# Hand-set engine order for the sample's MLP, four lasting two-bank PSUM tiles, down operands in three stages

## The chip, the cores and the metric

The kernel runs on one core of a Trainium2 chip. The metric is device time in microseconds (us) of one execution, the median of several runs. A core has engines with an instruction queue each: TensorE (PE in the profile, with its weight loads as PEld) multiplies matrices into PSUM, VectorE (DVE), ScalarE (ACT) and GpSimd (POOL) work elementwise, and SyncE (SP) issues most DMA transfers. Engines wait for each other on semaphores.

## The reference

One layer of an encoder is applied to two inputs with the same weights, a prompt of 512 rows and a sample of 1024 rows, width 1024. All is float32.

```
h = rmsnorm(x);  z = h @ w_in                       # q, k, v and two convolution inputs
a = window attention (128 to each side, relative bias, a sink logit per head)
c = silu(layernorm(depthwise conv over 31 rows of (ca * sigmoid(cb))))
x = x + concat(a, c) @ w_out
h = rmsnorm(x)
u = depthwise conv over 3 rows of (h @ w_up)         # 2 x 2816 columns: gate and value
x = x + (silu(u_gate) * u_value) @ w_down            # the MLP
y = rmsnorm(x)
```

The rows that matter here are the last four, for the sample.

## The kernel before

**Precision and products.** A float32 operand is split into a high part in the fast matmul format and a low part, the remainder (a cast on ACT, a subtraction on DVE or POOL). A product then takes three matmuls: high by high, high by low, low by high. Each is 128 x 128 by 128 x 512, or, for a transpose, 128 x 128 by 128.

**Until 907 us of the profiled execution** come the projections of both inputs (`proj`, L249 to L252: groups of matmuls into a PSUM bank, with `tick()` after each six, which lets other work be issued between), the convolution (`conv_items`: one scalar_tensor_tensor on DVE per tap, L292, which reads and writes an accumulator in a PSUM bank), attention (scores L501 to L524, values and their transposes L545 to L569), the convolution's norm (L604 to L624), the prompt's MLP (`up_half`: matmuls into two banks, then the centre tap on ACT, L778, and two outer taps on DVE, L774; `down`: L812 to L815) and the output projection (`out_half`, L640 to L645).

**PSUM.** In this part the PSUM is eight tiles of one bank (2 KB a partition), named a0 to a2, u0, u1, b0, b1 and c0 (L105). `use` (L109) says which letters a job may take: "step" (projections) takes a, u or b; the convolution's accumulator c; the prompt's up products u, its down products b. At 907 us this pool is closed, and a second pool of four tiles of two banks (`wide()`) serves the rest.

**The sample's MLP, from 907 us.** Both products use a scheme of seven products over halves, as Strassen's. The up product goes column block by column block: j from 0 to 21, each with a gate part x and a value part wy, each a wide tile with a left half L and a right half R. For a column the steps are `first` and `second` (into x left; `first` is also copied to a), `fourth` (x right), `sixth` then `seventh` (wy right, with sums u2 and u3 made from it on DVE, L915), `fifth` then `third` (wy left). Each is `prod`, 12 matmuls (L1042 to L1044). The rows of the normed x are transposed by `turned` (PE L965, cast on ACT L967, low part on DVE L918) in the start stage, and the up weights of column j come by DMA (`load_up`), are summed on DVE (`sums_up`, L918) and split (`split_up`: cast on ACT L1028, low part on POOL L918). Then come the depthwise convolution (centre on ACT L1140, two taps on DVE L1141 and L1142), the gate (tanh on ACT L1149, DVE L1159) and the product with the value (DVE L1161). The gated result of each pair of columns is written to DRAM in seven combinations (`ga`).

The down product is 77 steps, seven products over eleven pairs of columns. A step takes 12 matmuls (L1306 to L1308, `mm_down`), its operands are `ga` tiles and blocks of w_down, read again by `load_next`, with sums on DVE and splits on ACT, POOL and DVE (`operands`, made four steps ahead, `LEAD`). After each product `evacuate` adds the PSUM tiles into accumulators. `load_x1` loads the residual, `with_x` adds it. Behind the last product's steps stand the tail: add (L915), squares (`left_first` L1357, `finish` L1365), the reciprocal root on POOL (L1366 to L1368), scaling (L1372 to L1377) and the stores (L1378).

**What sets the order.** The code is written in an order, but the framework's scheduler rearranges the whole kernel's instructions on each engine before it is built (`schedule_with_timeline_sim=True`).

Of the kernel before, what the change touches and what calls it, by code (L numbers as in the profile page):

```python
# [15 lines left out]
P = 128  # L16
# [78 lines left out]

@with_exitstack
def tile_hybrid_encoder(ctx: ExitStack, tc: tile.TileContext, xs, rel_bias, norm_attn_g, w_in,
# [6 lines left out]
    ps_guard = tc.tile_pool(name="ps", bufs=1, space=bass.MemoryType.PSUM)  # L104
    ps = ps_guard.__enter__()  # L105
# [8 lines left out]
    def bank(job):  # L114
        return banks.tile([NT], among=use[job])
# [887 lines left out]

    def sums_up(j):
        if j < NJ:
            g0, g1, v0, v1 = (block_up(j, half, k) for half in range(2) for k in range(2))
            t = third_sum[j] = sb.tile([NT])
            sub(t[:], v1, v0, nc.gpsimd)
            sub(v0, v0, g0)
            sub(g0, v1, v0)  # L1010
            sub(g1, g1, g0)
# [70 lines left out]
    out_blocks(NB - 1, 1)  # L1082
# [3 lines left out]
    gFb = None  # L1086
# [4 lines left out]
    def wide():  # L1091
        return wide_banks.tile([W2])
# [5 lines left out]
    def first(j):  # L1098
        if j < NJ:
            s = st[j] = dict(x=wide(), a=sb.tile([NT]))  # L1100
            prod(s["x"][:, L], j, 1, True, True)
            nc.scalar.copy(s["a"][:], s["x"][:, L])
# [4 lines left out]
    def sixth(j):  # L1107
        s = st[j]
        s["wy"] = wide()
        s["u2"] = sb.tile([NT])  # L1110
        prod(s["wy"][:, R], j, 6, True, True)
        add(s["u2"][:], s["wy"][:, R], s["a"][:])

    def fourth(j, between=None):
        prod(st[j]["x"][:, R], j, 4, True, True, between)

    def seventh(j):
# [12 lines left out]

    def third(j):
        s = st[j]
        W = s["wy"][:, L]
        prod(W, j, 3, False, True)
        add(W, W, s.pop("u2")[:])

    def dwconv(src, f):
        w = lambda t: fw[:, t * 44 + f:t * 44 + f + 1]
        u = sb.tile([W2])
        nc.scalar.activation(u[:], src[:], AF.Identity, scale=w(1), bias=fb[:, f:f + 1])  # L1140
        nc.vector.scalar_tensor_tensor(u[:, 1:W2], src[:, 0:W2 - 1], w(0), u[:, 1:W2], op0=ALU.mult, op1=ALU.add)  # L1141
        nc.vector.scalar_tensor_tensor(u[:, 0:W2 - 1], src[:, 1:W2], w(2), u[:, 0:W2 - 1], op0=ALU.mult, op1=ALU.add)  # L1142
        return u

    def gate_part(j):
        s = st[j]
        ug = s["ug"] = dwconv(s.pop("x"), j)
        t = s["t"] = sb.tile([W2])
        nc.scalar.activation(t[:], ug[:], AF.Tanh, scale=0.5)  # L1149
# [3 lines left out]
    def value_part(j):  # L1153
        if j < 0:
            return
        p = j // 2
        s = st.pop(j)
        ug, t = s["ug"], s["t"]
        nc.vector.scalar_tensor_tensor(t[:], t[:], 1.0, ug[:], op0=ALU.add, op1=ALU.mult)  # L1159
        uv = dwconv(s.pop("wy"), NJ + j)  # L1160
        nc.vector.tensor_tensor(t[:], t[:], uv[:], op=ALU.mult)  # L1161
        del ug, uv
        s.clear()
        if j % 2 == 0:
            even[p] = t
            nc.sync.dma_start(ga[1, p][:], t[:, L])
            return
        e, x, y = even.pop(p), sb.tile([W2]), sb.tile([NT])
        for i, blk in ((2, L), (4, R)):
            nc.sync.dma_start(ga[i, p][:], t[:, blk])  # L1170
        add(x[:, R], e[:, R], t[:, R])
        sub(x[:, L], e[:, L], e[:, R], nc.gpsimd)
        sub(e[:, R], x[:, R], e[:, L])
        sub(y[:], t[:, L], e[:, R], nc.gpsimd)
        for i, b in ((5, x[:, R]), (7, x[:, L]), (6, e[:, R]), (3, y[:])):
# [3 lines left out]
    def halves():  # L1179
        while True:  # L1180
            t = wide()
            yield t, t[:, L]
            yield t, t[:, R]
            t = None

    two = halves()

    def turn(i):
        return turned(i, lambda: next(two))

    first(0)
    first(1)
    t = turn(4)
    next(t)
    second(0, t)
    for _ in t:
        pass
    t = turn(6)
    next(t)
    second(1, t)  # L1200
    for _ in t:
        pass
    split_up(0, 7)
    t = turn(7)
    next(t)
    fourth(0, t)
    for _ in t:
        pass
    split_up(1, 7)
    t = turn(5)  # L1210
    next(t)
    fourth(1, t)
    for _ in t:
        pass
    split_up(0, 5)
    for _ in turn(3):
        pass
    two.close()
    reserve(2)
    load_up(2, 0)  # L1220
    load_up(2, 1)
    split_up(1, 5)
    sixth(0)
    split_up(0, 3)
    sixth(1)
    split_up(1, 3)
    seventh(0)
    load_up(3, 0)
    seventh(1)
    load_up(3, 1)  # L1230
    fifth(0)
    split_up(2, 1, 2)
    sums_up(2)
    fifth(1)
    gate_part(0)
    third(0)
    split_up(2, 6, 4)
    value_part(0)
    first(2)
    gate_part(1)  # L1240
    third(1)
    split_up(2, 7, 5, 3)
    load_up(4, 0)
    load_up(4, 1)


    pr = {}
# [24 lines left out]
    hl = {}  # L1272

    def operands(i, p):

# [236 lines left out]
```

## Time and profile before

| | us |
|---|---|
| median of 3 runs | 1614.8 (1608.98 to 1616.14) |
| profiled execution, its whole time | 1616.81 |
| profiled execution, span from first to last instruction | 1615.0 |
| granted TensorE clock, mean | 0.984 |
| instructions on PE, DVE, ACT, POOL | 6907, 1681, 1358, 673 |
| HBM read, written | 158.84 MB, 48.51 MB |

The profile comes from one execution on the chip. A row of a group reads: line, engine, operation, output and inputs by the names of their buffers, shape, count; then the busy time of the group in us, the mean of one in ns, the time for which the engine was idle just before them, and the instruction that ended most of it. In rows by time the idle time and its releaser stand in square brackets. Matmuls overlap, so that the pitch, the time from one's start to the next one's start, is shorter than the duration shown for one.

### The profile page before, as it was taken

To read this page: it belongs to the slowest core of one execution; us is meant where nothing else is said; L and a number is where in the kernel's file an instruction comes from. 1 tells how busy PE (TensorE), PEld (TensorE's weight loads), DVE (VectorE), ACT (ScalarE), POOL (GpSimd) and SP (SyncE) were. 2 spreads that over 40 slices of the span, in tenths; PEclk is the share of its full clock that TensorE was granted. 3 is DMA by queue.
4 is the path that set the end of the run, shared out by engine and by line. 5 is a ranking of instruction groups with operands and counts; after the bars stand their busy time and mean duration, and the time that the engine had idled before them with its cause. 6 is when DMAs were issued, how large, how long until landed. Compare 5 with 4: busy or idle time off the path is not lost. (4 is left out here: it accounts for less than half of the span.)

```text
span 1615.0 us, 20218 instructions
## 1 busy us (share of the span) xinstructions
PE 1540.5 (95%) x6907; PEld 1243.8 (77%) x6907; DVE 1201.1 (74%) x1681; ACT 762.5 (47%) x1358; POOL 882.8 (55%) x673
## 2 busy tenths in 40 slices
PE   8999899999999999999999999999999999999995
PEld 6778788877877878888678767787777787878774
DVE  7999857749899987666656658777777776786685
ACT  4634656255556665555543334333343344344353
POOL 6641344157656866555622335656666664555586
PEclk9999999999999999999999979999999999999998
DMA  7572256274233333334482212333333324974512
GB/s 234 154 208 76 79 134 176 82 205 129 82 101 105 111 103 100 105 98 156 150 261 85 66 53 85 98 98 98 98 98 98 98 79 176 320 262 159 166 51 104
DMA packets 209772, 207.63 MB, mean 129 GB/s; under 512 B 11156, under 2 KB 150748, under 8 KB 209541
## 3 DMA queue, kind: packets, MB, share of 16 engines
q1 hardware_dynamic: 209669, 206.35, 40.6%
q8 instruction: 54, 0.88, 0.2%
q14 instruction: 49, 0.40, 0.1%
HBM read 158.84 MB, written 48.51 MB: 128 GB/s over the span
## 5 line engine op out<-in xcount | busy, mean ns | idle before, releaser
L918 POOL TENSOR_TENSOR q<-q,q 128x512 fp32r<-128x512 f32 x107 | 147.3, 1387 | 138.7 <-ACT q L1028 138.6
L1042 PE MATMUL w<-h,q 128*128 128x512 f32 x516 | 203.5, 397 | 10.8 <-DVE h L915 4.6
L143 POOL TENSOR_TENSOR q<-q,q 128x1024 fp32r<-128x1024 f32 x72 | 175.1, 2436 | 68.6 <-ACT q L142 37.5
L1044 PE MATMUL w<-h,q 128*128 128x512 f32 x516 | 201.2, 394 | 0.8 <-POOL q L918 0.8
L1043 PE MATMUL w<-h,q 128*128 128x512 f32 x494 | 194.6, 394 | 0.0
L918 DVE TENSOR_TENSOR h<-h,h 128x512 fp32r<-128x512 f32 (+1 forms) x126 | 137.8, 1136 | 45.6 <-DMA h<-in_w_down 28.0
L249 PE MATMUL u<-h,q 128*128 128x512 f32 x400 | 159.5, 399 | 3.6 <-DVE h L774 2.8
L250 PE MATMUL u<-h,q 128*128 128x512 f32 x400 | 159.0, 397 | 0.6 <-DVE h L211 0.6
L252 PE MATMUL u<-h,q 128*128 128x512 f32 x384 | 151.8, 395 | 2.0 <-POOL q L143 1.8
L918 POOL TENSOR_TENSOR h<-h,h 128x512 fp32r<-128x512 f32 x69 | 104.9, 1536 | 86.0 <-ACT h L922 61.4
L292 DVE SCALAR_TENSOR_TENSOR c<-c,cvw,c 128x512 f32<-128x512 f32 x184 | 137.9, 750 | 2.4
L922 ACT CAST h<-h 128x512 fp32r<-128x512 f32 x154 | 87.3, 618 | 110.6 <-DVE h L918 39.2
L1042 PEld LDWEIGHTS w<-h,q 128*128 128x128 f32 x516 | 97.5, 189 | 38.9 <-issue 8.1
L1307 PE MATMUL w<-h,h 128*128 128x512 f32 x296 | 117.9, 398 | 7.6 <-DVE h L918 7.6
L1308 PE MATMUL w<-h,h 128*128 128x512 f32 x308 | 122.1, 398 | 0.7 <-POOL h L918 0.7
L1306 PE MATMUL w<-h,h 128*128 128x512 f32 x308 | 122.0, 397 | 0.0
L1044 PEld LDWEIGHTS w<-h,q 128*128 128x128 f32 x516 | 97.4, 189 | 23.8 <-POOL q L918 1.7
L1028 ACT CAST q<-q 128x512 fp32r<-128x512 f32 x107 | 65.1, 620 | 105.8 <-PE w L1044 51.7
L142 ACT CAST q<-q 128x1024 fp32r<-128x1024 f32 x72 | 75.6, 1050 | 77.7 <-POOL q L143 44.3
L1043 PEld LDWEIGHTS w<-h,q 128*128 128x128 f32 x494 | 93.4, 189 | 20.2
L249 PE MATMUL b<-h,q 128*128 128x512 f32 x256 | 102.1, 399 | 1.9 <-DVE d L322 1.9
L250 PE MATMUL b<-h,q 128*128 128x512 f32 x256 | 100.7, 393 | 0.0
(398 smaller groups left out, 3957.5 us busy)
## 6 DMA issues: line engine op xcount, KB each, us to landing
q<-in_w_up SPq DMA_DIRECT2D x88, 512.0 KB
h<-in_w_down SPq DMA_DIRECT2D x110, 256.0 KB
h<-ga SPq DMA_DIRECT2D x77, 256.0 KB
ga<-q SPq DMA_DIRECT2D x66, 256.0 KB
q<-in_w_in SPq DMA_DIRECT2D x28, 512.0 KB
q<-in_x_sample SPq DMA_DIRECT2D x15, 512.0 KB
h<-qsd SPq DMA_DIRECT2D x24, 256.0 KB
q<-in_x_prompt SPq DMA_DIRECT2D x8, 512.0 KB
```

Source lines behind the costliest of these rows:

```text
L143: (nc.vector if dve else nc.gpsimd).tensor_tensor(lo[:], raw[:], hi[:].bitcast(F32), op=ALU.subtract)
L249: nc.tensor.matmul(out, whi[:, kc, :], hi[:], start=(kc == 0), stop=False)
L250: nc.tensor.matmul(out, whi[:, kc, :], lo[:], start=False, stop=False)
L252: nc.tensor.matmul(out, wlo[:, kc, :], hi[:], start=False, stop=(kc == KC - 1))
L292: nc.vector.scalar_tensor_tensor(acc[:], src(t), w(t), acc[:], op0=ALU.mult, op1=ALU.add)
L918: (eng or nc.vector).tensor_tensor(out, a, b, op=ALU.subtract)
L1042: nc.tensor.matmul(out, whi[:, s], hi[:], start=(start and c == 0), stop=False, **go)
L1043: nc.tensor.matmul(out, whi[:, s], lo[:], start=False, stop=False, **go)
L1044: nc.tensor.matmul(out, wlo[:, s], hi[:], start=False, stop=(stop and c == 3), **go)
L1306: nc.tensor.matmul(out, sh[:, c], th[:], start=(p == 0), stop=False)
L1307: nc.tensor.matmul(out, sh[:, c], tl[:], start=False, stop=False)
L1308: nc.tensor.matmul(out, sl[:, c], th[:], start=False, stop=(p == NPAIR - 1))
```

## The change

It has three parts.

1. *PSUM.* The class `Banks` makes four tiles of two banks, w0 to w3, which last for the whole kernel. In the early part the old bank names are halves of them: w0 is b0 and a2, w1 is b1 and c0, w2 is a0 and a1, w3 is u0 and u1. The MLP takes whole tiles. The closing of the first pool and the second pool go.
2. *Order.* From the scaling of the last block of rows to the end, the code stands under `tc.manual_schedule()`: each engine runs its instructions in the order in which they are written. That order is rewritten: the start stage with its transposes, the loop over the columns, and the tail. Before it, in the early part, the scheduler still sets the order.
3. *Down operands.* Sums are made two steps ahead of the low parts, casts one ahead, and the lows some steps ahead of the matmuls (`advance`, 4 steps, more toward the end). Loads begin in the last three columns, into slots that the raw up weights leave.

```diff
+class Banks:
+    NAMES = (("b0", "a2"), ("b1", "c0"), ("a0", "a1"), ("u0", "u1"))
+    def __init__(self, pool):
+        self.tiles = [pool.tile([P, 2 * NT], F32, tag=f"w{i}", name=f"w{i}", bufs=1) for i in range(4)]
+        self.free = [f"{k}{i}" for k, n in (("a", 3), ("u", 2), ("b", 2), ("c", 1)) for i in range(n)]
+        self.wides = list(range(4))
+    def bank(self, among):
+        name = next((b for b in self.free if b[0] in among), None)
...
+        i, h = next((i, pair.index(name)) for i, pair in enumerate(self.NAMES) if name in pair)
+        return Bank(self.free, name, self.tiles[i][:, h * NT:(h + 1) * NT])
+    def wide(self):
+        i = self.wides.pop(0)
+        return Bank(self.wides, i, self.tiles[i][:, :])
...
-    banks = Slots(ps, dict(a=(3, 2048), u=(2, 2048), b=(2, 2048), c=(1, 2048)))
+    banks = Banks(ps)
...
-    ps_guard.__exit__(None, None, None)
-    ps2 = ctx.enter_context(tc.tile_pool(name="ps2", bufs=1, space=bass.MemoryType.PSUM))
-    wide_banks = Slots(ps2, dict(w=(4, 4096)))
...
     def seventh(j):
         s = st[j]
-        s["u3"] = sb.tile([NT])
         prod(s["wy"][:, R], j, 7, False, True)
-        add(s["u3"][:], s["wy"][:, R], s.pop("a")[:])
+        u3 = s["u3"] = sb.tile([NT])
+        add(u3[:], s["wy"][:, R], s.pop("a")[:])
+        add(s["x"][:, R], s["x"][:, R], u3[:])
 
     def fifth(j):
         s = st[j]
-        W, Y = s["wy"][:, L], s["wy"][:, R]
-        prod(W, j, 5, True, True)
-        u3 = s.pop("u3")
-        add(Y, W, u3[:])
-        add(s["x"][:, R], s["x"][:, R], u3[:])
+        prod(s["wy"][:, L], j, 5, True, True)
+        add(s["wy"][:, R], s["wy"][:, L], s.pop("u3")[:])
...
+    def down_casts(k):
+        for x in list(hl[k]):
+            hi = sb.tile([NT], F32R)
+            nc.scalar.copy(hi[:], x[:])
+            hl[k].append(hi)
+    def down_lows(k):
+        a, b, ah, bh = hl[k]
+        p = steps[k][1]
+        al, bl = sb.tile([NT], F32R), sb.tile([NT], F32R)
+        sub(al[:], a[:], ah[:].bitcast(F32), None if p % 4 == 1 else nc.gpsimd)
+        sub(bl[:], b[:], bh[:].bitcast(F32), nc.gpsimd if p % 4 == 3 else None)
+        hl[k] = (ah, al), (bh, bl)
+    stages = [(2, down_sums), (1, down_casts), (0, down_lows)]
+    made = [0, 0, 0]
+    def advance(k):
+        while made[2] <= min(k, len(steps) - 1):
+            m = made[2]
+            for n, (dist, stage) in enumerate(stages):
+                while made[n] <= min(m + dist, len(steps) - 1):
+                    stage(made[n])
+                    made[n] += 1
...
-        make(k + (LEAD if k else 1))
+        if k:
+            advance(k + 4 + max(0, k - 55) // 2)
...
+    order = tc.manual_schedule()
+    order.__enter__()
+    scaled(NB - 1)
...
     for j in range(2, NJ):
+        last = j == NJ - 1
         for half in range(2):
             load_up(j + 3, half)
+        if j >= NJ - 3:
+            sb.free.extend(raws.free[:2])
+            del raws.free[:2]
+            load_next(2 if j < NJ - 1 else 6)
+        value_part(j - 1)
         split_up(j + 1, 1, 2)
         fourth(j)
+        gated(j - 1)
+        sixth(j)
+        if not last:
+            t3_up(j + 1)
+        gated_sums(j - 1)
+        second(j)
         sums_up(j + 1)
-        sixth(j)
-        value_part(j - 1)
-        second(j)
+        split_up(j + 1, 4, 6)
         seventh(j)
-        split_up(j + 1, 6, 4)
+        gate_centre(j)
+        split_up(j + 1, 7, 5, 3)
         fifth(j)
...
+        gate_taps(j)
+        gate_tanh(j)
+        if last:
+            advance(0)
             down_step(0)
-        first(j + 1)
...
+            advance(1)
+        else:
+            first(j + 1)
+            keep_first(j + 1)
         third(j)
-        split_up(j + 1, 7, 5, 3)
-    sb.free.extend(raws.free)
     value_part(NJ - 1)
+    gated(NJ - 1)
+    gated_sums(NJ - 1)
...
+    for tt in (2, 3):
+        squares(tt, soon(tt), (0,))
+        nc.vector.tensor_tensor(cut(o11, tt), cut(o11, tt), fins[0][:, L], op=ALU.mult)
     for tt in range(2):
         add(cut(o12, tt), z[:, tt * NT:(tt + 1) * NT], cut(o12, tt))
-        finish(tt, (cut(o11, tt), cut(o12, tt)), False)
-    del z
+        squares(tt, soon(tt))
+        rstd(tt)
+    for tt in range(2):
+        finish(tt, soon(tt))
+    z = None
     for tt in (2, 3):
-        left_first(tt)
-        z = wide()
+        z = banks.wide()
         for p in range(NPAIR):
-            mm_down(z[:, L], 3, p, tt)
+            mm_down(z[:, L], base + p, tt)
         add(cut(o12, tt), z[:, L], cut(o12, tt))
-        finish(tt, (cut(o11, tt), cut(o12, tt)), True)
-        del z
+        squares(tt, soon(tt), (1,))
+        rstd(tt)
+        finish(tt, soon(tt), True)
+        z = None
```

Not shown: the parts of `gate_part` and `value_part` become functions of their own (centre, taps, tanh, `gated`, `gated_sums`) with the same operations; `squares`, `rstd` and `finish` hold what `left_first` and `finish` held; the residual's loads and those of the final gain stay at their steps, two of them one step earlier.

More of the change, by code (lines that the diff above doesn't have):

```diff
@@ new lines, in tile_hybrid_encoder @@
+    next(turns)
+    second(0, turns)
+    split_up(0, 7)
+    second(1, turns)
+    split_up(1, 7)
+    fourth(0, turns)
+    split_up(0, 5)
+    split_up(1, 5)
+    fourth(1, turns)
+    for _ in turns:
+        pass
+    two.close()
+    sixth(0)
+    split_up(0, 3)
+    split_up(1, 3)
+    reserve(2)
+    for half in range(2):
+        load_up(3, half)
+    sixth(1)
+    seventh(0)
+    gate_centre(0)
+    seventh(1)
+    gate_centre(1)
+    split_up(2, 1, 2)
+    fifth(0)
+    gate_taps(0)
@@ L1419, in tile_hybrid_encoder @@
+    gate_tanh(0)
+    fifth(1)
+    sums_up(2)
+    third(0)
+    split_up(2, 4, 6)
+    value_part(0)
+    first(2)
+    keep_first(2)
+    gated(0)
+    gate_taps(1)
+    gate_tanh(1)
+    third(1)
+    split_up(2, 7, 5, 3)
+    for half in range(2):
+        load_up(4, half)
     for j in range(2, NJ):
+        last = j == NJ - 1
         for half in range(2):
             load_up(j + 3, half)
+        if j >= NJ - 3:
[3 more added lines that the diff above has]
+        value_part(j - 1)
```

321 lines of the change are left out of this document (139 added, 182 removed).

## The prediction

> **What bounds the kernel now.** I read the busy shares first, then the busy time by stretch, then the rows that stop the matrix engine inside the stretches the change touches.
>
> ```profile
> span 1615.0 us, 20218 instructions
> ...
> PE 1540.5 (95%) x6907; PEld 1243.8 (77%) x6907; DVE 1201.1 (74%) x1681; ACT 762.5 (47%) x1358; POOL 882.8 (55%) x673
> ...
> DVE  7999857749899987666656658777777776786685
> ```
>
> TensorE (PE) is busy 95% of the span, so a change that takes no matmul away can give back only the rest, and every new stop of PE is paid in full. VectorE (DVE) is next, and its row of 40 slices (40 us each) stands at 8 or 9 in ten of the first sixteen. The busy times by stretch (columns: length, PE, weight load, DVE, ACT, POOL, granted clock, DMA share, GB/s):
>
> ```profile
> 0.00:907.00 907.00, 871.38 (x4056) 708.83 (x4057) 695.84 (x1177) 471.99 (x905) 476.15 (x375) 0.99 0.44 132
> 907.00:960.00 53.00, 48.83 (x212) 37.43 (x213) 26.91 (x37) 20.25 (x36) 17.72 (x15) 0.84 0.16 50
> 960.00:1060.00 100.00, 95.04 (x398) 75.95 (x397) 75.84 (x76) 38.53 (x53) 55.53 (x41) 0.97 0.27 85
> 1060.00:1360.00 300.00, 295.68 (x1273) 237.73 (x1272) 215.97 (x222) 121.52 (x167) 181.37 (x133) 1.00 0.32 105
> 1360.00:1390.00 30.00, 27.53 (x117) 21.32 (x116) 25.20 (x24) 15.55 (x24) 16.14 (x11) 1.00 0.71 245
> 1390.00:1599.00 209.00, 202.04 (x858) 162.51 (x856) 154.33 (x141) 89.02 (x164) 128.85 (x89) 0.98 0.50 168
> 1599.00:1615.00 16.00, 0.00 (x0) 0.00 (x0) 7.03 (x9) 5.67 (x12) 7.07 (x11) 0.66 0.40 149
> 1300.00:1340.00 40.00, 40.00 (x174) 32.34 (x174) 32.25 (x31) 15.89 (x22) 23.62 (x18) 1.00 0.21 73
> 1420.00:1430.00 10.00, 6.33 (x21) 4.71 (x20) 8.82 (x10) 5.11 (x10) 4.95 (x4) 0.83 0.72 251
> 100.00:200.00 100.00, 93.20 (x442) 75.60 (x441) 88.47 (x179) 49.55 (x118) 29.52 (x20) 1.00 0.36 104
> 500.00:600.00 100.00, 96.23 (x441) 77.31 (x441) 94.47 (x167) 63.12 (x121) 71.80 (x49) 1.00 0.32 101
> ```
>
> In 1300 to 1340 PE never idles, and 174 matmuls take 40 us: 0.23 us is the pitch of one, the unit of everything below. What a stretch loses is its length less matmuls times 0.23. Up to 907 us run the projections, the convolution, attention and the prompt's feed-forward net; from there the sample's MLP. In the MLP the losses are 8.5 us (960 to 1060), 7.2 (to 1360), 3.1 (to 1390), 11.7 (to 1599) and 16 behind the last matmul. All that the hand-set order can win lies in these 46 us and in the start stage, 907 to 960, where PE also ran at clock 0.84.
>
> **The PSUM tiles.** The diff reads as a change to the MLP, but the class Banks now serves the whole kernel. Before, the early part had eight tiles of one bank; now each bank is half of a tile of two: b0 with a2, b1 with c0 (the convolution's accumulator), a0 with a1, u0 with u1. I traced the semaphore waits of the two built programs to the instruction that releases each. The waits are kept by tile, not by bank: an access to one half waits for earlier accesses to the other, with no data between them. Before, only the MLP had that, in its wide tiles. One such wait can be seen there, in the transposes of the start stage, which fill the two halves of a tile in turn:
>
> ```profile
> 927.96 1.28 ACT L967 CAST h<-w 128x512 fp32r<-128x512 f32 x2 [0.78 <-PE w L965]
> 928.58 1.39 DVE L918 TENSOR_TENSOR h<-w,h 128x512 fp32r<-128x512 f32 x2 [0.67 <-ACT h L967]
> ...
> 929.33 0.44 PE L965 MATMUL w<-ident,q 128*128 128x128 f32 x2 [0.70 <-DVE h L918]
> ```
>
> The built program of the changed kernel has some 370 waits of this kind on PE, about 330 of them before 907 us, where the kernel before has none. Their causes run on DVE and ACT at these prices (instructions by shape, 0 to 907 us; mean ns behind the comma):
>
> ```profile
> L292 DVE SCALAR_TENSOR_TENSOR c<-c,cvw,c 128x512 f32<-128x512 f32 x184 | 137.9, 750 | 2.4
> ...
> L774 DVE SCALAR_TENSOR_TENSOR h<-u,fw,h 128x511 f32<-128x511 f32 x88 | 65.4, 743 | 13.1 <-ACT h L778 12.4
> ...
> L815 DVE TENSOR_TENSOR q<-b,q 128x512 f32<-128x512 f32 x88 | 59.9, 684 | 17.8 <-PE b L814 17.2
> ...
> L778 ACT ACTIVATE h<-u,vecs,fw 128x512 f32<-128x512 f32 x44 | 34.1, 774 | 21.4 <-PE u L252 6.7 <-PE a L559 4.0 <-DMA catd<-h 3.0
> ...
> L548 DVE TENSOR_TENSOR h<-a,h 128x512 fp32r<-128x512 f32 x42 | 28.4, 681 | 5.2 <-ACT h L547 5.1
> L547 ACT CAST h<-a 128x512 fp32r<-128x512 f32 x49 | 27.8, 578 | 13.6 <-PE a L545 12.5 <-POOL h L285 1.0
> ```
>
> A wait costs PE what is left of its cause when the matmuls placed between are done, each worth 0.23 us. Counted in the built order:
> - Projections into b1 against the convolution's steps in c0: 56 waits. A step takes 0.75 us, about 0.8 with the handover. Behind 22 of them fewer than four matmuls (0.92 us) stand between, some meet two steps in a row: about 1.0 each, 22 us.
> - Projections into u1 against the taps of u0 (and the reverse): 43 waits on a chain of the centre, 0.77, and two taps, 0.74 each, 2.3 us. 19 of them lack cover, 0.8 on average: 15 us.
> - Attention's transposes and scores, the prompt's down products, the output projection and the early transposes: about 105 waits of 0.58 to 0.74 us that are mostly covered, a quarter us each: 25 us.
>
> That is 62 us; the same count finds 4 in the kernel before, so 58 are new. It adds stops that may overlap: one stop of PE gives the next cause time to finish. On the transposes of the start stage of the kernel before, the count is a quarter above what the trace shows, so about 47. Against that, DVE reaches each step late where it is 88 to 94% busy. I take **+50**. Bounds: half the scaled count, +24; all of the first two kinds uncovered, 56 × 0.8 + 43 × 0.8 + 25 − 4 = +100. No row allows a gain here: nothing is removed.
>
> On the other side stands the Trainium skill, "PSUM — Partial Sum Buffer", section "PSUM bank collisions raise a hardware error": accesses need a semaphore by bank and quadrant of partitions, and two engines on different banks ran clean. By that rule no wait between two halves would be needed and this term would be 0, the time that of the third rival below; the row at 929.33 shows a stop of this kind all the same, so I do not follow it.
>
> **The main loop.** PE's order per column is now fourth, sixth, second, seventh, fifth, first of the next column, third. Fifth writes the left half of the tile whose right half DVE reads for the sum u3 right after seventh: a wait by tile again, with nothing of PE's between. Before, another product often stood there. The price is a DVE add and the handover, seen here:
>
> ```profile
> 1048.06 0.68 DVE L915 TENSOR_TENSOR h<-w,h 128x512 f32<-128x512 f32 x1
> ...
> 1048.79 0.80 PE L1042 MATMUL w<-h,q 128*128 128x512 f32 x1 [3.24 <-DVE h L915]
> ...
> 1425.35 0.50 PE L1307 MATMUL w<-h,h 128*128 128x512 f32 x1 [3.67 <-DVE h L918]
> ```
>
> The last matmul of seventh ends about 0.4 after its start (the row at 1598.42 below), the add takes 0.68, the handover 0.05; PE would have gone on after 0.23: 0.9 us, in 20 columns, 18 us. In every other column DVE is still in the sums of the next column (0.85 us each, below): half a us more, ten times, 5. With 3 for filling the first columns the loop loses 26 instead of 8.5 + 7.2 = 15.7: **+10**, between −6 (half of each add covered) and +21 (1.7 a column). PE's waits on its own earlier matmuls go; they stop nothing in 1300 to 1340, so 0. The start stage keeps its transposes and has 12 such waits instead of 10, one more in it at 0.7: +1.
>
> **Into the down products.** Before step 2's low part DVE now has the last column's value part and sums in written order (1060 to 1340 us, by shape):
>
> ```profile
> L1141 DVE SCALAR_TENSOR_TENSOR q<-w,fw,q 128x1023 f32<-128x1023 f32 x28 | 35.8, 1280 | 33.1 <-ACT q L1140 33.1
> ...
> L915 DVE TENSOR_TENSOR w<-w,h 128x512 f32<-128x512 f32 x42 | 29.1, 693 | 15.0 <-PE w L1044 14.8
> ...
> L1159 DVE SCALAR_TENSOR_TENSOR q<-q,q 128x1024 f32<-128x1024 f32 x14 | 24.8, 1772 | 16.9 <-ACT q L1149 16.9
> ...
> L918 DVE TENSOR_TENSOR q<-q 128x512 f32<-128x512 f32 x28 | 23.7, 854 | 0.0
> ...
> L1161 DVE TENSOR_TENSOR q<-q,q 128x1024 f32<-128x1024 f32 x14 | 20.8, 1488 | 0.2
> ```
>
> 0.69 + 1.77 + 2 × 1.28 + 1.49 + two sums of about 0.85, with the low itself some 9 us. Queued behind it on POOL is the other low, behind that on SP the loads that follow a write of the gated rows. PE has step 1, 12 × 0.23 = 2.8 us: a stop of about 7. At 1425.35 PE stood 3.67 us and the clock of those 10 us was 0.83, 1.7 us lost; the same again makes 8.5, against 3.1 now: **+5** (0 to +9, by whether the value part starts earlier).
>
> **The down loop.** Sums are made two steps ahead, casts one, and the loads of x1 and the final gain keep their place behind the operands' loads. Before, they ran early, inside the stretch where the DMA share is 0.72:
>
> ```profile
> PE w L1307 <- DVE h L918: 7.6, 4, 3.7
> ```
>
> These four stops (7.6 us, the longest 3.7) came from lows whose operands landed late. I keep 4 of the 11.7 us lost: **−8** (−10 to 0).
>
> **The tail.**
>
> ```profile
> 1597.48 0.63 ACT L1357 ACTIVATE q<-q 128x512 f32<-128x512 f32 x1 [3.96 <-DMA out_sample<-q]
> ...
> 1598.42 0.40 PE L1308 MATMUL w<-h,h 128*128 128x512 f32 x1
> ...
> 1599.53 1.28 DVE L915 TENSOR_TENSOR q<-w,q 128x512 f32<-128x512 f32 x2
> ...
> 1604.95 0.68 DVE L915 TENSOR_TENSOR q<-w,q 128x512 f32<-128x512 f32 x1
> ...
> 1608.09 0.68 DVE L915 TENSOR_TENSOR q<-w,q 128x512 f32<-128x512 f32 x1
> ```
>
> The last matmul ends at 1598.8, the end is at 1615.0: 16.2. The adds of blocks 0 and 1, then 2 and 3, stood behind a square that waited for a store. In the written order only the last block's chain is left, and from its add at 1608.09 to the end are 6.9 us: 7.2 with the handover, **−9** (−9.5 to −4).
>
> **Sum.** +50 +10 +1 +5 −8 −9 = +49. The late terms alone are −1, between −15 and +15 (their ends do not all fall together). The profiled execution took 1616.8 us, span 1615.0, which is 2.0 above the median of the runs; 1616.8 + 49 less these 2.0 is **1664**. Its own range, early from +24 to +75: 1638 to 1690.
>
> **Rivals.**
> - *DVE becomes the bound.* 40 convolution steps now wait in DVE's queue for a group of six matmuls in the other half (6 × 0.23 = 1.4 us), up to 55 us in about 400 us where the rows of 100 and 500 us leave DVE some 40 free. Everything behind them on DVE, taps and lows, is then late for PE too: another 45 on top, 1614.8 + 49 + 45 = **1709**. For it: 94.47 in 500 to 600. Against: the steps can slip behind each other without PE needing them soon.
> - *The waits fall into idle time.* Already before, PE idles 907 − 871 = 36 us in the early part. If most of the new waits end inside such gaps, the early term is +8; with a loop of −5, a transition at 0, −10 and −9 the time is 1614.8 + 8 − 24 = **1599**. It decides as soon as the early term is below 24. Against it: 41 of the waits stand with less PE work than their price before them.
> - *The waits cost nothing*, because two banks are independent in fact and their releases come early: early 0, late −1, **1614**. Against it the row at 929.33.
>
> **How the numbers follow.** My forecast 0.63; DVE as bound 0.16; waits in idle time 0.13; no cost 0.08. About 0.5%, 8 us, is what a measurement of this kernel can tell from no change. Faster 0.13, same 0.08, slower 0.79. The range reaches from just above the idle-time rival, 1603, to just beyond the DVE rival, 1713, and so leaves out about half of each rival's own spread, some 0.15 in all.
>
> **What would show it.** Right: the MLP starts about 50 us later than 907; the early waits name PE u or b behind L292's and L774's successors on DVE; fifth's first matmul idles 0.9 us in each column behind DVE's add; a stop of about 7 us at the second down step; no stop of 3.7 among the first down steps; 7 us behind the last matmul. Wrong: an MLP that begins within 15 us of 907, or idle before fifth below 0.4 us. If DVE is above 95% in the early slices with PE below 85%, the first rival holds.

## The result, and the profile after

The changed kernel takes 1869.77 us (1867.32 to 1872.19) against 1613.39 us (1608.98 to 1616.14) of the kernel before on the same chip: a ratio of 1.1592, 95% interval 1.1557 to 1.1627. It is slower by 256 us; the forecast was slower by 49, with 1713 as the upper end of the range.

From the page of the changed kernel: the span, the busy time of each engine, and by 40 slices DVE's busy share and the granted TensorE clock in tenths.

```profile
span 1865.5 us, 20314 instructions
...
PE 1628.0 (87%) x6907; PEld 1281.9 (69%) x6907; DVE 1198.5 (64%) x1681; ACT 763.7 (41%) x1358; POOL 893.5 (48%) x673
...
DVE  7765554647378777655556654666666666556897
...
PEclk8999988998989899999999999899999999899998
```

The counts of instructions are the same, and DVE works as long as before (1198.5 against 1201.1). PE is busy 87.5 us longer with the same 6907 matmuls, most of it because it ran part of them at a lower clock (row PEclk). The rest of the 250.5 us of longer span is idle time of PE. DVE's first sixteen slices, at 8 or 9 in ten of them before, now reach 8 once.

Where the stages begin is read from the line of the first matmul of the up products and that of the down products (durations in ns, then the first and the last start). Lines of the changed kernel are 33 to 37 higher than those of the kernel before. After:

```profile
L1079 PE MATMUL w<-h,q x528: 387/393/775, 1098.0 to 1623.2; 128*128 128x512 f32 x176
L1308 PE MATMUL w<-h,h x292: 387/393/796, 1615.7 to 1854.0; 128*128 128x512 f32 x146
```

Before:

```profile
L1042 PE MATMUL w<-h,q x516: 387/393/795, 906.9 to 1388.9; 128*128 128x512 f32 x172
L1306 PE MATMUL w<-h,h x308: 387/393/628, 1362.7 to 1598.0; 128*128 128x512 f32 x154
```

| stretch | before, us | after, us | difference | predicted |
|---|---|---|---|---|
| to the first MLP product | 906.9 | 1098.0 | +191.1 | +50 |
| from there to the first down matmul | 455.8 | 517.7 | +61.9 | +11, and part of the transition's +5 |
| down products, to the last matmul | 235.7 | 238.8 | +3.1 | rest of the +5, and -8 |
| behind the last matmul's start | 16.6 | 11.0 | -5.6 | -9 |

The stretches do not hold quite the same work. In the changed kernel 24 matmuls of the early part come after its first MLP product, where the kernel before has none; and 12 of the up products' matmuls come after its first down matmul, against 36 before. At 0.23 us each that is 5.5 us twice: for equal work the differences are about +197, +51, +9 and -6.

The busy time by stretch of the changed kernel (the columns are those of the prediction):

```profile
0.00:1098.00 1098.00, 939.30 (x4028) 733.95 (x4028) 684.55 (x1168) 478.13 (x902) 472.90 (x375) 0.94 0.36 109
1098.00:1200.00 102.00, 82.46 (x366) 64.26 (x365) 58.07 (x72) 34.21 (x55) 34.30 (x27) 0.92 0.23 70
1200.00:1600.00 400.00, 371.01 (x1543) 295.99 (x1542) 264.15 (x274) 140.58 (x201) 230.27 (x162) 0.97 0.27 88
1600.00:1650.00 50.00, 36.08 (x132) 27.50 (x132) 30.01 (x29) 18.51 (x29) 19.92 (x13) 0.83 0.41 146
1650.00:1855.00 205.00, 199.10 (x846) 160.24 (x844) 158.71 (x137) 89.36 (x166) 132.12 (x91) 0.98 0.53 179
```

In the early part PE's busy time goes from 871.4 to 939.3 us (+68), and its idle time from 35.6 to 158.7 (+123). Those two make the 191. The granted clock is 0.94 instead of 0.99: the trace's clock records have it at half for 133 us of this stretch (10 before), and PE was busy in 110 us of them (10 before), so that about (110 - 10) / 2 = 50 of the 68 us are the clock's. The other 18 fit the end of each run of matmuls: the last one shows its own 0.39 us instead of the pitch of 0.23, and there are 147 stops of more than 0.05 us instead of 41 (an estimate, 106 x 0.16 = 17). What PE waited for in the early part of the changed kernel (time in all, times, longest; the nine largest of many):

```profile
PE w L282 <- DVE w L325: 17.2, 18, 3.8
PE w L282 <- DVE h L807: 10.0, 8, 2.5
PE w L534 <- DVE s L537: 10.0, 9, 2.0
PE w L845 <- DVE q L848: 9.2, 9, 1.8
PE w L534 <- DMA h<-qsd: 8.9, 1, 8.9
PE w L282 <- DVE h L333: 8.7, 2, 8.4
PE w L578 <- DVE s L537: 6.8, 9, 1.2
PE w L534 <- DVE h L602: 5.1, 2, 4.5
PE w L637 <- DMA h<-cvd: 4.7, 3, 2.5
```

The first two rows are the projections against the convolution's steps and against the taps: 17 and 10 us, where the prediction had counted 22 and 15. They are 27 us, beside 123 us of added idle time. The rest is spread over many waits, among them some for DMA and some for data that the matmul really needs.

The loop of the changed kernel by time. First PE at the start of fifth in column 3; all odd columns are alike:

```profile
1214.07 0.50 PE L1079 MATMUL w<-h,q 128*128 128x512 f32 x1 [0.78 <-DVE h L948]
```

Then DVE, and PE at the start of fifth, in column 4; the even columns from 6 on are alike:

```profile
1231.68 1.29 DVE L951 TENSOR_TENSOR q<-q,q 128x512 f32<-128x512 f32 x2 [1.18 <-POOL q L951]
1233.08 2.38 DVE L951 TENSOR_TENSOR q<-q 128x512 f32<-128x512 f32 x2
1235.37 0.68 DVE L948 TENSOR_TENSOR h<-w,h 128x512 f32<-128x512 f32 x1
...
1236.11 0.50 PE L1079 MATMUL w<-h,c 128*128 128x512 f32 x1 [2.43 <-DVE h L948]
```

Fifth stops behind the DVE add of seventh, as forecast, 0.78 us in odd columns. In even ones the add (1235.37) stands behind four subtractions, the first of which itself waited 1.18 us for POOL: 2.43 us of idle time instead of the 1.4 predicted. Such a stop can be followed by half the clock. Here is the next one of the even columns, then the windows of the clock records, 3.41 us long, around the stop that ends at 1236.11 and around this one:

```profile
1278.57 0.65 PE L1079 MATMUL w<-h,q 128*128 128x512 f32 x1 [2.45 <-DVE h L948]
...
1234.38:1237.79 3.41, 1.68 (x7) 1.42 (x8) 2.27 (x4) 1.98 (x3) 1.60 (x2) 1.00 0.26 96
1237.79:1241.21 3.42, 3.42 (x16) 2.82 (x16) 2.00 (x3) 1.92 (x4) 3.35 (x3) 1.00 0.36 105
1275.34:1278.75 3.41, 0.96 (x5) 0.48 (x4) 3.17 (x5) 0.81 (x2) 1.34 (x2) 1.00 0.71 266
1278.75:1282.17 3.42, 3.42 (x9) 2.64 (x9) 0.49 (x1) 3.08 (x5) 3.33 (x3) 0.50 0.00 0
```

The first stop lies across the edge of two windows, PE is busy for 1.68 of the 3.41 us, and the clock stays at 1.00. The second lies within one window, PE is busy for 0.96 us, and the next window has a clock of 0.50, which costs 1.7 us. Seven of the nine stops of 2.4 us in the loop are followed by such a window. In the whole trace of the changed kernel it goes by PE's busy share of a window at full clock: 40 windows with a share of at most 45% are followed by half the clock, 445 with at least 47% are not. Over the traces of all runs the two kinds overlap, from 44 to 60%.

The Trainium skill ("TensorE: Matmul & The Clock Gate", section "What's actually happening") has an activity window of about 3.4 us that runs freely. The rows agree with that. They also show that a stop of 2.45 us, shorter than the window, can be enough.

At the transition to the down products PE stops before the first down matmul, for a cast (the changed kernel by time):

```profile
1615.75 0.80 PE L1308 MATMUL w<-h,h 128*128 128x512 f32 x1 [5.47 <-ACT h L1281]
```

and again behind step 1, for the two low parts of step 2:

```profile
1632.07 0.80 PE L1309 MATMUL w<-h,h 128*128 128x512 f32 x1 [5.08 <-DVE h L951]
1634.87 0.79 PE L1310 MATMUL w<-h,h 128*128 128x512 f32 x1 [2.00 <-POOL h L951]
```

The tail of the changed kernel by time:

```profile
1854.50 0.39 PE L1310 MATMUL w<-h,h 128*128 128x512 f32 x1
1855.24 0.68 DVE L948 TENSOR_TENSOR q<-w,q 128x512 f32<-128x512 f32 x1
...
1857.78 0.75 DVE L1503 SCALAR_TENSOR_TENSOR q<-q,s,q 128x512 f32<-128x512 f32 x1 [1.86 <-POOL s L1495]
...
1858.44 0.68 DVE L948 TENSOR_TENSOR q<-w,q 128x512 f32<-128x512 f32 x1
```

The last matmul ends at 1854.9, but its add starts at 1858.44: the written order puts block 2's scaling (1857.78) ahead of it on DVE, and that waited for POOL.

### The profile page after: what moved, and what is told of

The parts are those of the page before. It is cut to its first block, busy times and chain, and to the rows that moved or that the text cites. A ratio compares the mean times of both kernels' runs of the same rounds, so it can differ in the third digit from the quotient of the medians.

```text
span 1865.5 us, 20314 instructions
## 1 busy us (share of the span) xinstructions
PE 1628.0 (87%) x6907; PEld 1281.9 (69%) x6907; DVE 1198.5 (64%) x1681; ACT 763.7 (41%) x1358; POOL 893.5 (48%) x673
## 5 line engine op out<-in xcount | busy, mean ns | idle before, releaser
L282 PE MATMUL w<-h,q 128*128 128x512 f32 x688 | 291.4, 424 | 47.0 <-DVE w L325 17.2
L283 PE MATMUL w<-h,q 128*128 128x512 f32 x688 | 284.0, 413 | 0.8 <-DVE h L244 0.8
L285 PE MATMUL w<-h,q 128*128 128x512 f32 x672 | 275.0, 410 | 0.0
L1079 PE MATMUL w<-h,q 128*128 128x512 f32 x528 | 216.6, 410 | 36.1 <-DVE h L948 30.4
L951 POOL TENSOR_TENSOR q<-q,q 128x512 fp32r<-128x512 f32 (+1 forms) x111 | 142.7, 1303 | 176.4 <-ACT q L1065 175.5
L1081 PE MATMUL w<-h,q 128*128 128x512 f32 x528 | 212.9, 403 | 0.0
L1080 PE MATMUL w<-h,q 128*128 128x512 f32 x514 | 208.6, 406 | 0.0
L282 PEld LDWEIGHTS w<-h,q 128*128 128x128 f32 x688 | 138.0, 201 | 93.5 <-DVE w L325 23.8
L325 DVE SCALAR_TENSOR_TENSOR w<-c,cvw,w 128x512 f32<-128x512 f32 x184 | 138.3, 752 | 32.9 <-PE w L285 26.6
L283 PEld LDWEIGHTS w<-h,q 128*128 128x128 f32 x688 | 138.2, 201 | 28.2 <-DVE h L244 1.1
L285 PEld LDWEIGHTS w<-h,q 128*128 128x128 f32 x672 | 134.4, 200 | 30.1
L951 DVE TENSOR_TENSOR h<-h,h 128x512 fp32r<-128x512 f32 (+1 forms) x107 | 126.9, 1231 | 35.4 <-ACT h L1281 16.7
L1079 PEld LDWEIGHTS w<-h,q 128*128 128x128 f32 x528 | 102.9, 195 | 67.9 <-DVE h L948 32.3
L951 POOL TENSOR_TENSOR h<-h,h 128x512 fp32r<-128x512 f32 x61 | 98.0, 1625 | 80.3 <-ACT h L1281 26.2
L1308 PE MATMUL w<-h,h 128*128 128x512 f32 x292 | 117.5, 402 | 5.5 <-ACT h L1281 5.5
L1081 PEld LDWEIGHTS w<-h,q 128*128 128x128 f32 x528 | 103.2, 195 | 24.0
L1080 PEld LDWEIGHTS w<-h,q 128*128 128x128 f32 x514 | 100.7, 196 | 21.7
L948 DVE TENSOR_TENSOR w<-w,h 128x512 f32<-128x512 f32 x64 | 44.7, 699 | 108.4 <-PE w L1081 107.7
```

What stands on the lines that cost most here:

```text
L282: nc.tensor.matmul(out, whi[:, kc, :], hi[:], start=(kc == 0), stop=False)
L283: nc.tensor.matmul(out, whi[:, kc, :], lo[:], start=False, stop=False)
L285: nc.tensor.matmul(out, wlo[:, kc, :], hi[:], start=False, stop=(kc == KC - 1))
L325: nc.vector.scalar_tensor_tensor(acc[:], src(t), w(t), acc[:], op0=ALU.mult, op1=ALU.add)
L951: (eng or nc.vector).tensor_tensor(out, a, b, op=ALU.subtract)
L1079: nc.tensor.matmul(out, whi[:, s], hi[:], start=(start and c == 0), stop=False, **go)
```

## The experiments

Each is one execution with a profile beside runs of the kernel before on the same chip (1610 to 1619 us over the four chips used), but for the last, which was timed in rounds. "First product" is the start of the first MLP product.

### Is it the PSUM tiles, and which

*One-bank tiles early.* The early part gets its eight one-bank tiles back, the MLP keeps the lasting wide ones, and the order stays set by hand.

```diff
-    banks = Banks(ps)
+    banks = EarlyBanks(ps)          # NAMES: one name per tile, tiles of len(names) banks
...
+    ps_guard.__exit__(None, None, None)
+    ps2 = ctx.enter_context(tc.tile_pool(name="ps2", bufs=1, space=bass.MemoryType.PSUM))
+    banks = Banks(ps2)
```

> The changed kernel with one edit: until the MLP the PSUM is again eight tiles of one bank, closed before the MLP, which then takes the four tiles of two banks; hand-set order and down operands as in the changed kernel. Theory T (the early loss of some 190 us is made by waits between the two banks of one tile, and by the half clock behind those stops): the first MLP product starts at 907 us, give or take 15, against 1098 in the changed kernel, and the time is about 1870 - 190 = 1680 us. Rival O (the hand-set order of the MLP no longer lets the scheduler run work of the MLP under the early part, or delays the early part's loads): the first MLP product stays near 1098 and the time near 1870 us. Clock early: T 0.99, O 0.92.

Measured: first product 906.9, time 1668.6 us. Theory T holds in what it forecast, 201 us are back; whether the waits themselves made the loss is asked below. What is left over the kernel before, 55 us, comes from the hand-set order and the down operands. The row of the first MLP product:

```profile
L1088 PE MATMUL w<-h,q x528: 387/393/766, 906.9 to 1424.9; 128*128 128x512 f32 x176
```

*The kernel before with the PSUM part alone* (`Banks` in the whole kernel, order left to the scheduler).

> The kernel before with the PSUM part of the change alone: four lasting tiles of two banks in the whole kernel, all order left to the scheduler, down operands as before. Theory T: the early part is as slow as in the changed kernel, first MLP product at about 1095 us, time 1614 + 190 = about 1804 us. Rival O: first MLP product at about 907, time 1614 +- 10 us. Between them (both matter): about 1000 and 1710.

Measured: first product 1101.3, time 1818.8 us. The PSUM part alone makes the early loss; the hand-set order has no share in it. The same row here:

```profile
L1075 PE MATMUL w<-h,q x516: 387/393/797, 1101.3 to 1592.1; 128*128 128x512 f32 x172
```

*One pair alone.* One-bank tiles, but b1 with c0.

```diff
+    NAMES = (("a0",), ("a1",), ("a2",), ("u0",), ("u1",), ("b0",), ("b1", "c0"))
```

> As the run with one-bank tiles, but b1 and c0 (the convolution's accumulator) share one tile of two banks in the early part, the other six banks alone. Theory T with the shares of the prediction's count (22 of 62 us for the projections against the convolution): a third of the 190 us, first MLP product at about 970, time about 1745 us. Rival C (the convolution's pair makes nearly all of it, since the other pairs rarely are in use together): first product above 1050, time above 1820. Rival O: no difference from the run with one-bank tiles.

Measured: first product 1056.6, time 1818.1 us. That is Rival C, but for 2 us of its bound on the time: this one pair costs 150 us. The same with u0 and u1 as the pair:

> As the run with one-bank tiles, but u0 and u1 (the prompt's up products) share a tile in the early part. By the prediction's count, 15 us of stops, with the clock's half periods some 25: first MLP product at about 932, time about 1694 us. Rival (the other work of PE hides them): first product within 8 us of 907, time within 8 of 1669.

Measured: first product 1021.2, time 1783.5 us, 115 us more, where the count gave 25. 150 and 115 do not add up to the 201 us of all four pairs, and with the u pair time is lost before the prompt's MLP begins (the first output projection at 324.9 instead of 273.9 us). Neither fits a price per wait.

*Taking the pair's partner away.* In the changed kernel, first c0 beside a bank that nobody takes (so the early part has one bank less, and b0 shares with b1), then the convolution's accumulator in SBUF:

```diff
-    NAMES = (("b0", "a2"), ("b1", "c0"), ("a0", "a1"), ("u0", "u1"))
+    NAMES = (("b0", "b1"), ("a2", "c0"), ("a0", "a1"), ("u0", "u1"))
...
-        self.free = [f"{k}{i}" for k, n in (("a", 3), ("u", 2), ("b", 2), ("c", 1)) for i in range(n)]
+        self.free = [f"{k}{i}" for k, n in (("a", 2), ("u", 2), ("b", 2), ("c", 1)) for i in range(n)]
```

```diff
-            acc = bank("conv")
+            acc = sb.tile([NT])
```

> The changed kernel with other halves: c0 (the convolution's accumulator) shares its tile with a2, which nobody takes any more, and b0 shares with b1; lasting tiles and all else as in the changed kernel. Theory T (the convolution's steps on DVE and the projections' groups on PE hold each other up through the tile they share, worth the 150 us that the run with this pair alone lost): first MLP product at about 1098 - 150 = 950, time about 1720 us. Rival N (with one bank less and b0 beside b1 the other pairs take over the loss): first product above 1040, time above 1810.

> The changed kernel with the convolution's accumulator in SBUF instead of bank c0, so that b1 has no neighbour in use; pairs as in the changed kernel. Theory T: the same 150 us go, first MLP product at about 950, time about 1720 us. Rival A (the loss is the price of the waits alone, 17 us idle behind the convolution's steps and the clock's share of it, some 30 us): first product above 1060, time above 1830.

Measured: first products 1164.2 and 1143.2, times 1951.6 and 1915.2 us. Theory T fails in both. The values lie beyond the bounds of the rivals (above 1040 and 1060), but neither rival said that the loss would grow. The first run changes two things at once, the neighbour and the number of banks, and does not part them. In the second, the convolution's steps cost more, which I had not allowed for (by shape, the changed kernel with the accumulator in SBUF):

```profile
L325 DVE SCALAR_TENSOR_TENSOR h<-c,cvw,h 128x512 f32<-128x512 f32 x184 | 186.7, 1015 | 3.2
```

1015 ns instead of the 750 of the accumulator in PSUM. So this run says nothing clean on the tiles.

### Waits or order

The scheduler plans the order of the early part, and knows the waits by tile when it does. So another tile layout gives another order on every engine: in the traces, the one-bank run has the early order of the kernel before on PE, DVE, ACT and POOL (compared by line and shape, but for a few matmul records), and the changed kernel that of the run with the PSUM part alone, and these two orders differ on all four. To part the two, the next runs take one-bank tiles, where no wait between halves exists, and hold each engine's early instructions in the order that the scheduler had chosen for another kernel. The edges add no semaphore, and the three traces show the order that was asked for on all four engines.

```diff
+    for e in told:                    # engine -> names of its instructions, in that order
+        there = [made_[f"I-{n}"] for n in told[e] if f"I-{n}" in made_]
+        for one, two_ in zip(there, there[1:]):
+            tc.add_manual_dep(two_, one.name, mybir.DependencyInfo(mybir.DependencyClass.NoSync,
+                              mybir.DependencyReason.DATA), reason="order")
     order = tc.manual_schedule()
```

> One-bank tiles early (no wait between halves there), but every engine's early instructions held in the very order that the scheduler chose for the run with the u pair alone. Theory W (the waits between the two halves stop PE and DVE): they are gone, so the first MLP product comes back to within 20 us of 907, time about 1680 us. Theory O (the scheduler plans another order for the whole early part when tiles carry two banks, and that order is slow in itself): first product at about 1020 as with the pair, time about 1783 us.

> The same with the early order that the scheduler chose for the run with the convolution's pair alone. Theory W: first MLP product within 20 us of 907, time about 1680 us. Theory O: first product at about 1055, time about 1818 us. Half way, about 980 and 1745, if the waits and the order share it.

> The same with the early order of the changed kernel itself, all four pairs. Theory W: first MLP product at about 907 to 925, time about 1680 us. Theory O: first product at about 1098, time about 1868 us.

| order of | with its waits: first product, time | without them: first product, time | early loss that stays |
|---|---|---|---|
| the u pair | 1021.2, 1783.5 | 999.2, 1761.3 | 92 of 114 us |
| the convolution's pair | 1056.6, 1818.1 | 1048.6, 1808.4 | 142 of 150 us |
| the changed kernel | 1098.0, 1869.8 | 1059.1, 1820.0 | 152 of 191 us |

Theory O holds in all three: most of the loss is in the order itself, and the waits between halves add 22, 8 and 39 us to it (the 8 is no more than runs of one kernel differ by, 1610.1 to 1618.8 us on one chip). The run with the changed kernel's order and no such waits, its first MLP product and its early part as one window:

```profile
L1091 PE MATMUL w<-h,q x528: 387/393/766, 1059.1 to 1574.7; 128*128 128x512 f32 x176
...
0.00:1059.00 1059.00, 920.74 (x4055) 737.74 (x4055) 681.95 (x1177) 477.41 (x904) 475.60 (x375) 0.94 0.38 113
```

And what PE waits for in it (lines are 45 higher than in the kernel before):

```profile
PE e L604 <- ACT h L592: 16.5, 7, 3.5
PE e L649 <- DMA h<-cvd: 14.8, 3, 12.1
PE e L857 <- DVE q L860: 10.9, 9, 4.0
PE e L546 <- DMA h<-qsd: 9.6, 2, 8.8
PE e L605 <- DVE h L593: 8.8, 6, 2.3
```

The idle time is 138.3 against 35.6 us before, and PE is busy 49 us longer (920.7 against 871.4), about 42 of it by the clock, counted as above. None of these waits is between halves. Four are for data that the matmul needs, such as attention's values for the cast of the transposed attention weights (L604) or the convolution's norm for rows that come back from DRAM (L649); the prompt's down products wait for the add that frees their bank (L857). In the run with one-bank tiles and their own order (lines 42 higher) the first of these is small:

```profile
PE e L291 <- DVE h L816: 2.8, 1, 2.8
...
PE e L601 <- ACT h L589: 1.9, 1, 1.9
```

The row of L601 there is that of L604 above: 1.9 us, once, against 16.5 us in seven. For this consumer the traces show how the orders differ: on PE, between a group of transposed weights and the next values product stand 10 matmuls in the median in the order planned for two-bank tiles, and 23 in the one planned for one-bank tiles (50 places in each). For the other rows I have not shown it; that their consumers too stand nearer behind their producers, or behind a producer that is late on its own engine, is a reading.

*A plan changed in another way.* One-bank tiles, no order imposed, the accumulator in SBUF:

> One-bank tiles early, no order imposed, and the convolution's accumulator in SBUF instead of bank c0: a change to the scheduler's plan that adds no wait between halves. Theory W: within 20 us of the one-bank run, 1669. Theory O in its strong form (any change of the plan costs, because the kernel's constants fit the one plan): first MLP product after 960, time above 1720 us.

Measured: first product 1046.8, time 1808.1 us. It looks like the strong form, but the convolution's steps took 1151 ns in it (184 of them, 211.1 us against 138.0, and the other 104 took 110.3 against 78.3), so DVE had 105 us more to do; whether any change of the plan costs as much stays open. Beside it, the run above with the accumulator in SBUF and the other pairs in place started its first product at 1143.2, another 96 us later.

*Which engine's order.*

> One-bank tiles early, and only PE held in the early order of the changed kernel; the scheduler plans the other engines around it. If PE's order carries the loss of 151 us that the whole order made without its waits: first MLP product at about 1059, time about 1820 us. If the order of DVE and the others carries it: within 30 us of 1669.

> The opposite: DVE, ACT, POOL and SP held in the early order of the changed kernel, PE free for the scheduler. If PE's order carries the loss: within 40 us of 1669. If the others' order carries it, or PE is planned into the same order again: about 1800 us or above.

Measured: with PE's order alone first product 1034.0, time 1793.3 us; with the other engines' alone 1070.0 and 1832.5 us. Either carries most of the loss, so that it cannot be put down to one engine. A likely reason, not shown, is that the scheduler plans the free engines around the held ones. The opposite test, the good order over two-bank tiles, was not run.

### The hand-set order

*First of the next column between seventh and fifth*, in the changed kernel:

```diff
+        if not last:
+            first(j + 1)
+            keep_first(j + 1)
         fifth(j)
```

> The changed kernel with one edit in the column loop: the first product of the next column stands between seventh and fifth instead of behind fifth. Theory F (fifth stops for the DVE add of seventh, because both write or read halves of one tile: 0.8 us idle in ten columns, 2.4 us in ten others, and there half a clock window of 3.4 us, 1.7 us, behind it): 8 + 24 + 17 = 49 us less, time about 1820 us, early part unchanged. Rival G (the stop only moves: the product put there waits for PSUM or for its split operand, or third stops instead): less than 15 us gained, above 1855 us.

Measured: 1837.1 us, 33 less. Between the theories: fifth's stops are gone between 1200 and 1560 us, and the half clock with them (1.00), but third now stands directly behind fifth and waits for the DVE add that reads fifth's result (waits of PE, 1200 to 1560 us):

```profile
PE w L1079 <- DVE w L948: 13.5, 17, 0.8
```

*Fourth between seventh and fifth*, on the one-bank version, with first left between fifth and third; the next column's sums go behind the add of seventh, and the value part's taps of the column before behind sixth.

```diff
-        value_part(j - 1)
+        value_start(j - 1)
         split_up(j + 1, 1, 2)
-        fourth(j)
+        sixth(j)
+        value_taps(j - 1)
         gated(j - 1)
-        sixth(j)
...
-        sums_up(j + 1)
-        split_up(j + 1, 4, 6)
         seventh(j)
+        sums_up(j + 1)
+        split_up(j + 1, 6, 4)
+        fourth(j)
+        gate_sum(j)
         gate_centre(j)
```

> The one-bank run with the new column order alone (fourth between seventh and fifth, the next column's sums behind the DVE add of seventh; start stage and transition as in the changed kernel). Theory F: the loop's 46 us lost between 1000 and 1400 fall to below 12, time about 1669 - 38 = 1631 us. Rival G (the stop moves): above 1650 us.

Measured: 1620.0 us, 49 less than the one-bank run. In the one-bank run PE idled 29.1 us of 400 in the loop, at clock 0.97:

```profile
1000.00:1400.00 400.00, 370.94 (x1543) 295.91 (x1542) 264.08 (x274) 140.71 (x201) 230.45 (x162) 0.97 0.27 88
```

With the new column order it never idles in these 340 us of the loop:

```profile
1000.00:1340.00 340.00, 340.00 (x1478) 277.18 (x1477) 249.41 (x262) 134.40 (x192) 206.49 (x156) 1.00 0.30 97
```

*All three edits.* In addition the start stage's transposes go in turn to two tiles, and the operands of the first five down steps are made early in the last column.

```diff
-            t = banks.wide()
-            yield t, t[:, L]
-            yield t, t[:, R]
+        t = [banks.wide() for _ in range(2)]
+        while True:
+            for half in (L, R):
+                for x in t:
+                    yield x, x[:, half]
...
+        if last:
+            advance(4)
```

> The run with one-bank tiles early, and three edits in the hand-set order: fourth stands between seventh and fifth and the sums of the next column behind the DVE add of seventh; the transposes of the start stage alternate between two tiles instead of the two halves of one; the operands of the first five down steps are made in the last column ahead of the column's taps. Theory F (the +55 us of the one-bank run against the kernel before are these stops by tile and by DVE's order: 46 us in the loop, 13 in the start stage, 20 at the transition): 1669 - 40 - 8 - 15 = about 1605 us. Rival G (the stops move to other products of the column): above 1640 us.

> The version with all three edits, timed in rounds against the kernel before: 1595 us as in the one look, ratio 0.988 +- 0.003, so that it is faster than both kernels. If the one look was a lucky run: within 0.5% of 1613.

Measured: 1595.2 us in the single execution, 1597.8 us in rounds (1594.0 to 1599.9), a ratio to the kernel before of 0.9897, 95% interval 0.9861 to 0.9932. It is faster than both kernels, than the one before by about 1%. The two further edits are worth some 25 us together; they were not run apart. In the start stage, the transposes waited 1.1 us in three stops, against 10.3 us in nine in the changed kernel.

## Why the prediction was wrong

- *Direction and place*: right. The early part, through the shared PSUM tiles, makes most of the loss, and the PSUM part alone does it.
- *The step that failed* is "The PSUM tiles", +50. It priced only the waits between two halves of a tile and took the rest of the early part as it was ("No row allows a gain here: nothing is removed", and the kernel before's own stops left in place). The waits themselves cost 39 us in the changed kernel's order, within the term's bounds; by pair the count did less well (22 counted and 8 measured for the convolution's pair, 15 and 22 for the u pair, each in its own order). What was left out is that the scheduler plans the whole early part anew around such waits, and that this order costs 152 us even without them. The built order was at hand, and all its waits could have been counted, not only those of the new kind.
- *The clock* was costed at the transition alone. In the early part it is about 50 of the 191 us.
- *DVE as the bound*: not so. DVE was busy for 684.6 of 1098 us, against 695.8 of 907 before. Convolution steps did wait for projections in the other half, as this rival said (45.0 us in 25 waits of DVE), but DVE had the time.
- *Waits in idle time*, and *no cost*: not so; the early term is far above 24.
- *The loop*, +10: the mechanism was right, fifth behind the add of seventh, the size too small. Odd columns cost 0.78 (predicted 0.9), even ones 2.43 instead of 1.4, and behind seven of those nine stops the half clock costs another 1.7. From 1200 to 1600 us PE lost 400 - 1543 x 0.23 = 45 us, where 26 were predicted for the loop.
- *The start stage*, +1: one more stop of 0.7 was predicted; its transposes waited 10.3 us in nine stops, against 3.1 in six before.
- *The transition*, a stop of 7 at step 2: found as 5.08 and 2.00, but a stop of 5.47 ahead of it, for the first step's cast, was not foreseen, and the clock was 0.83 over 50 us. These 50 us lost 50 - 132 x 0.23 = 20 us, where 8.5 were predicted.
- *The down loop*, -8 and *the tail*, -9: too hopeful. From 1650 to 1855 us PE still lost 205 - 846 x 0.23 = 10 us, against 11.7 before. The tail gained 5.6, since block 2's scaling still stands ahead of the last add.

## What to carry to other kernels

Where a scheduler sets the order, a change to what shares a tile is a change to the order of everything it plans; compare the two built orders, and count all waits that lose their cover, not only the new ones. Where the order is written by hand, place between a product and the next write to its tile as much matrix work as the slowest reader takes with its queue ahead of it, and then look at what stands directly behind the product that was moved.

## What the runs showed of the hardware

- Stops of 2.4 us can halve the clock for the next 3.4 us or leave it alone. In the changed kernel's trace the clock halved behind each of the 40 full-clock windows of 3.41 us in which PE was busy at most 45% of the time, and behind none of the 445 in which it was busy 47% or more. Spread stops cost about 50 us of clock in the early part on top of 123 us of idle time.
- A scalar_tensor_tensor of 128 x 512 with its accumulator in PSUM took 750 ns, with the accumulator in SBUF 1015 in one kernel and 1151 in another.
